# x2's token tiles 1 to 3 turned for the gate by VectorE and DMAs over DRAM instead of by TensorE

## The chip, the cores and the metric

One core of a Trainium2 chip runs the kernel. The metric is the device time of one execution in microseconds (us), as the median of several runs; lower is better.

## What is computed

One layer of a small transformer over 512 tokens (`SEQ`) of width 1024 (`D_MODEL`). Two attentions of 8 heads each are computed, normalised, gated and projected by `w_out`; the part that matters here comes after them:

```python
x = x + jnp.concatenate([y_sb, y_mb], axis=-1) @ w_out[i]
ple_gate = jax.nn.sigmoid(rmsnorm(x, g_ple[i]) @ w_ple_gate[i])
x = x + (p[i] @ w_ple[i]) * ple_gate
return rmsnorm(x, g_final)
```

The gate's matmul contracts over the 1024 features of x, so the features have to lie on partitions, while the sum in the line above it leaves the tokens on partitions. That turn of x is what the change is about.

## The kernel before

The 512 tokens are four tiles t = 0 to 3 of 128 tokens. `x2[0]` is one SBUF tensor `[128, 4, 1024]` (it prints as `x_2542`), tokens of a tile on partitions. Every matmul is made of three (`mul3`): both operands are split into a high and a low part in f32r, and high by high, high by low and low by high are accumulated in PSUM.

The kernel ends in this order:

- The output projection of the last heads. `out_step` fills a PSUM bank with half a tile (512 features), and `end_out` (line 422) adds it to `x2` on VectorE. The last three halves come from the generator `rest`: (tile 2, half 1) in a bank of the tag `tp`, (3, 0) and (3, 1) in the two banks that `bank()` gives out (`pj`, 2 buffers).
- Between them TensorE turns tile 0: `h2(0, 0)` and `h2(0, 1)`. `h2(t, c)` turns four blocks of 128 by 128 (`tr`, line 73: a TensorE transpose against the identity `idf`, into PSUM), and `split` makes the high part (`part_hi`, line 82, a cast on ScalarE) and the low part (`part_lo`, line 88, a subtraction on VectorE) of `H2[t]`, printed as `h`.
- The gate, tile by tile. `gate_steps` runs 24 matmuls of 128x512 for each half n of a tile (8 blocks k by 3) into a bank `pj`. After the first 12 of them `h2(t + 1, n)` turns half of the next tile. `end_gate` takes the sigmoid on ScalarE (line 890, out of PSUM, which frees the bank) and on VectorE multiplies by the loaded `pl` (line 891) and adds to `x2` (line 894). Then tile t is normalised and stored (lines 923 and 158).
- Tile 3 is cut into 512, 256 and 256 columns, and the kernel ends with its normalisation and its store.

TensorE runs in the order of the program text. ScalarE, VectorE, GpSimd and SP (SyncE, which issues all loads by `load`, line 158) are put in order by a scheduler when the kernel is built; on the chip each engine runs its own list in that order, and an instruction that waits holds all that stand behind it. `raw` is a pool of three buffers of `[128, 1024]` f32 through which all weights are loaded; the gate's weights are the last to use it. `pl_d` is a DRAM tensor to which the kernel stores a product early and from which it reads `pl` back here.

```python
        for n in range(2):
            ps = bank()
            gate_steps(t, ps, range(4), n * S, (n + 1) * S)
            h2(t + 1, n)
            gate_steps(t, ps, range(4, KT), n * S, (n + 1) * S)
            end_gate(t, n * S, (n + 1) * S, ps, r, pt[n])
```

Of the kernel before, what the change touches and what calls it, by code (L numbers as in the profile page):

```python
# [8 lines left out]
F32 = mybir.dt.float32  # L9
F32R = mybir.dt.float32r  # L10
# [5 lines left out]
P = 128  # L16
S = 512
DM = 1024
KT = DM // P
# [4 lines left out]
NT = S // P  # L24
# [10 lines left out]
def layer(ctx, tc, x, xT, pT, w_qkz, w_v, gcols, g_final, w_out, w_ple, w_gate, out):  # L35
# [12 lines left out]
    nc = tc.nc  # L48

    cst = ctx.enter_context(tc.tile_pool(name="cst", bufs=1))  # L50
    raw = ctx.enter_context(tc.tile_pool(name="raw", bufs=3))
# [4 lines left out]
    at = ctx.enter_context(tc.tile_pool(name="at", bufs=2))  # L56
    dram = ctx.enter_context(tc.tile_pool(name="dram", bufs=1, space=bass.MemoryType.DRAM))
# [8 lines left out]
    def bank():  # L66
        return pp.tile([P, S], F32, name="pj", bufs=2)
# [4 lines left out]
    def tr(ps, src):  # L72
        nc.tensor.transpose(ps, src, idf)  # L73

    def mul3(ps, ah, al, bh, bl, start, stop):
        mm(ps, ah, bh, start, False)
        mm(ps, ah, bl, False, False)
        mm(ps, al, bh, False, stop)

    def part_hi(hi, src, scale=None):  # L80
        if scale is None:
            nc.scalar.copy(hi, src)  # L82
        else:
            nc.scalar.activation(hi, src, AF.Copy, scale=scale)  # L84

    def part_lo(hi, lo, src, scale=None):
        if scale is None:
            nc.vector.tensor_sub(lo, src, hi.bitcast(F32))  # L88
        else:
            nc.vector.scalar_tensor_tensor(lo, src, scale, hi.bitcast(F32), op0=OP.mult, op1=OP.subtract)  # L90

    def split(hi, lo, src, scale=None):
        part_hi(hi, src, scale)
        part_lo(hi, lo, src, scale)
# [10 lines left out]
    def pop_w():  # L105
        if wq:
            hi, lo = wq.popleft()
            hi()
            if pend:
                pend.pop(0)()  # L110
            pend.append(lo)
        elif pend:
            pend.pop(0)()
# [8 lines left out]
    def tick(w=True):  # L122
        if w:
            pop_w()
        if fq:
            pop_f()
        for e in list(late):
            e[0] -= 1
            if e[0] <= 0:
                late.remove(e)  # L130
                e[1]()
# [25 lines left out]
    def load(tile_, src):  # L157
        nc.sync.dma_start(tile_, src)  # L158
# [259 lines left out]
    x2 = [None]  # L418
# [345 lines left out]
    for h in range(2 * NH):  # L764
        if h == 0:
            front(0)
        else:
            b = h - 1
# [47 lines left out]
    b = 2 * NH - 1  # L816
# [44 lines left out]
    def rms2(t):  # L861
        junk = at.tile([P, DM], BF16, name="junk", tag="o")
        ss = sm.tile([P, 1], F32, name="ss")
        nc.scalar.activation(junk, x2[0][:, t, :], AF.Square, accum_out=ss)  # L864
        r = sm.tile([P, 1], F32, name="r2")
        rstd(r, ss, DM, 1)
        return r

    H2 = {}

    def h2(t, c):
        if c == 0:
            H2[t] = [at.tile([P, KT, P], F32R, name=f"h2{i}", tag="AC"[i]) for i in range(2)]
        tp = pp.tile([P, 4, P], F32, name="tp2", tag="tp", bufs=2)
        for k in range(4):
            tr(tp[:, k, :], x2[0][:, t, (4 * c + k) * P:(4 * c + k + 1) * P])
        split(H2[t][0][:, 4 * c:4 * c + 4, :], H2[t][1][:, 4 * c:4 * c + 4, :], tp)

    def gate_steps(t, ps, ks, a, b):
        n, a, b = a // S, a % S, (b - 1) % S + 1  # L880
        for k in ks:
            while k not in wg or (t == 0 and n == 0 and (wq or pend) and k == KT - 1):
                pop_w()
            mul3(ps[:, :b - a], H2[t][0][:, k, :], H2[t][1][:, k, :], wg[k][n][0][:, a:b], wg[k][n][1][:, a:b],
                 k == 0, k == KT - 1)
            tick()

    def end_gate(t, a, b, ps, r, pt, between=None):
        gs = at.tile([P, S], F32, name="tmp")
        nc.scalar.activation(gs[:, :b - a], ps[:, :b - a], AF.Sigmoid, scale=r)  # L890
        nc.vector.tensor_mul(gs[:, :b - a], gs[:, :b - a], pt)
        if between:
            between()
        nc.vector.tensor_add(x2[0][:, t, a:b], x2[0][:, t, a:b], gs[:, :b - a])
# [10 lines left out]
    flush_late()  # L905
    while wq or pend:
        pop_w()
    for t in range(NT - 1):
        r = rms2(t)
        pt = [at.tile([P, S], F32, name="pl", tag="ph", bufs=2) for n in range(2)]  # L910
        for n in range(2):
            load(pt[n], pl_d[t, :, n * S:(n + 1) * S])
        for n in range(2):
            ps = bank()
            gate_steps(t, ps, range(4), n * S, (n + 1) * S)
            h2(t + 1, n)
            gate_steps(t, ps, range(4, KT), n * S, (n + 1) * S)
            end_gate(t, n * S, (n + 1) * S, ps, r, pt[n])
        r3 = rms2(t)
        for n in range(2):  # L920
            ns = slice(n * S, (n + 1) * S)
            ot = at.tile([P, S], F32, name="ot", tag="plo", bufs=2)
            nc.vector.scalar_tensor_tensor(ot, x2[0][:, t, ns], r3, gf[:, ns], op0=OP.mult, op1=OP.mult)
            load(out[t * P:(t + 1) * P, ns], ot)

    t = NT - 1
# [10 lines left out]
    def gate_cut(c, between=None):  # L937
        a, b = cuts[c]
        ps = bank()
        gate_steps(t, ps, range(KT), a, b)  # L940
        end_gate(t, a, b, ps, r, pt[a // S][:, a % S:a % S + b - a], between)
        return x2[0][:, t, a:b]
# [59 lines left out]
```

## Time and profile before

| | |
|---|---|
| time, median of 3 runs | 353.77 us (353.69 to 353.99) |
| time of the profiled execution | 353.86 us |
| its span, first to last instruction | 352.1 us |
| granted TensorE clock, mean | 0.993 |
| TensorE matmul (PE) busy | 343.4 us, 98% |
| TensorE weight load (PEld) busy | 287.4 us |
| VectorE (DVE) busy | 276.8 us, 79% |
| ScalarE (ACT) busy | 221.0 us, 63% |
| GpSimd (POOL) busy | 19.9 us, 6% |

The span is what the profile shows; the execution's own time is 1.76 us longer. Matmuls are pipelined: two that follow each other overlap in the records, so a stretch of them is read from start to start. PEld is the load of a matmul's weights, which runs beside the matmul ahead of it. SPq rows are DMA issues of SP.

### The profile page before, as it was taken

Reading aid. Unit: us, or ns where it says so; the run is one execution under the profiler, and the core shown is the slowest. Engines: PE = TensorE matmul, PEld = TensorE weight load, DVE = VectorE, ACT = ScalarE, POOL = GpSimd, SP = SyncE. Lnnn points to the kernel's source line nnn. Section 1 sums busy time; section 2 is a strip of 40 time slices with the busy share of each in tenths; the row PEclk is TensorE's granted clock in tenths of the full one; section 3 lists DMA queues with packets and bytes.
Section 4 is the critical chain, followed back from the end, with each engine's and each line's share of the span. In section 5 each row is a group of like instructions: output and inputs, shape, how many; then the busy total and the mean of one; then the engine's idle time right before and its main releaser. Section 6 shows DMA issues by size and latency. Waiting matters only on the chain.

```text
span 352.1 us, 4888 instructions
## 1 busy us (share of the span) xinstructions
PE 343.4 (98%) x1712; PEld 287.4 (82%) x1712; DVE 276.8 (79%) x564; ACT 221.0 (63%) x416; POOL 19.9 (6%) x43
## 2 busy tenths in 40 slices
PE   8999999999999999999999999999999999999991
PEld 7888888888888888888888888888888887888891
DVE  4887789788979797898489889989899877343554
ACT  4876857666766565685587499797776571343241
POOL 2023000000000000000000100000000010010011
PEclk9999999999999999999999999999999999999997
DMA  7997724303130313111005311122713750021221
GB/s 214 417 353 246 266 71 168 119 2 119 43 139 0 121 50 130 60 62 61 2 0 190 110 55 61 66 60 74 286 60 116 235 189 2 25 94 61 89 90 60
DMA packets 15464, 40.17 MB, mean 114 GB/s; under 512 B 1616, under 2 KB 1872, under 8 KB 15440
## 3 DMA queue, kind: packets, MB, share of 16 engines
q1 hardware_dynamic: 15296, 39.60, 32.1%
q8 instruction: 13, 0.21, 0.2%
q10 hardware_dynamic: 144, 0.26, 0.2%
q14 instruction: 11, 0.09, 0.1%
HBM read 35.66 MB, written 4.19 MB: 113 GB/s over the span
## 4 chain that ended last, share of the span: by engine, by line
PE 86%; DVE 4%; DMA 4%; issue 3%; ACT 1%; POOL 1%; SPq 0%; POOLq 0%; ACTq 0%; DVEq 0%
PE pj L70 64%; PE av L70 7%; PE sc L70 7%; PE tp L73 6%; DMA raw<-in_w_gate_dram 2%; PE tp L70 2%; DVE x L422 1%; DMA rawh<-in_pT_dram 1%; DVE wg L90 1%; POOL r L99 1%; SPq L158 0%; DVE wu L88 0%; ACT wg L84 0%; ACT junk L864 0%; POOLq L998 0%
## 5 line engine op out<-in xcount | busy, mean ns | idle before, releaser
L70 PE MATMUL pj<-hTh,wu 128*128 128x512 f32 x384 | 134.5, 401 | 0.0
L70 PEld LDWEIGHTS pj<-hTh,wu 128*128 128x128 f32 x384 | 72.2, 188 | 13.0
L70 PE MATMUL pj<-hTl,wu 128*128 128x512 f32 x192 | 75.1, 391 | 0.0
L82 ACT CAST wu<-raw 128x512 fp32r<-128x512 f32 x80 | 46.8, 619 | 24.7 <-PE pj L70 20.8
L88 DVE TENSOR_TENSOR wu<-raw,wu 128x512 fp32r<-128x512 f32 x80 | 53.3, 689 | 1.4 <-ACT wu L82 1.0
L70 PE MATMUL pj<-wg,h 128*128 128x512 f32 (+1 forms) x216 | 46.2, 371 | 0.0
L70 PEld LDWEIGHTS pj<-wg,h 128*128 128x128 f32 x216 | 37.0, 188 | 6.9
L70 PEld LDWEIGHTS pj<-hTl,wu 128*128 128x128 f32 x192 | 36.3, 189 | 5.1
L88 DVE TENSOR_TENSOR plo<-tp,ph 128x512 fp32r<-128x512 f32 (+1 forms) x48 | 28.5, 594 | 6.5 <-ACT ph L82 6.0
L82 ACT CAST ph<-tp 128x512 fp32r<-128x512 f32 (+1 forms) x48 | 24.5, 511 | 13.4 <-PE tp L73 13.3
L70 PE MATMUL pj<-wu,yh 128*128 128x512 f32 x96 | 30.9, 402 | 0.0
L70 PE MATMUL pj<-wu,hTh 128*128 128x512 f32 x96 | 30.1, 395 | 0.0
L621 DVE TENSOR_TENSOR_SCAN inc<-A,own 128x512 f32<-128x512 f32 (+3 forms) x32 | 24.7, 809 | 5.4 <-ACT A L616 5.4
L73 PEld LDWEIGHTS tp<-idf,C 128*128 128x128 f32 x160 | 20.4, 140 | 6.1
L73 PE MATMUL tp<-idf,C 128*128 128x128 f32 x160 | 25.2, 272 | 0.0
L70 PE MATMUL sc<-K,QH 128*128 128x512 f32 (+1 forms) x64 | 19.8, 323 | 0.0
L70 PEld LDWEIGHTS pj<-wu,hTh 128*128 128x128 f32 x96 | 17.3, 188 | 3.1
L70 PE MATMUL av<-ph,v 128*128 128x512 f32 (+1 forms) x64 | 19.7, 309 | 0.0
L658 ACT ACTIVATE C<-A,nm 128x512 f32<-128x512 f32 (+3 forms) x32 | 17.8, 558 | 3.1 <-DVE nm L654 3.0
L298 DVE TENSOR_TENSOR ev<-pj,rx 128x512 f32<-128x512 f32 x24 | 16.4, 684 | 3.9 <-PE pj L70 3.7
L70 PE MATMUL av<-plo,v 128*128 128x512 f32 (+1 forms) x64 | 19.1, 324 | 0.0
L70 PE MATMUL sc<-K,QL 128*128 128x512 f32 (+1 forms) x64 | 19.0, 323 | 0.0
(137 smaller groups left out, 557.2 us busy)
## 6 DMA issues: line engine op xcount, KB each, us to landing
raw<-in_w_qkz_dram SPq DMA_DIRECT2D x24, 512.0 KB, 3.4
raw<-in_w_v_dram SPq DMA_DIRECT2D x8, 512.0 KB, 3.3
raw<-in_w_out_dram SPq DMA_DIRECT2D x8, 512.0 KB, 3.7
raw<-in_w_gate_dram SPq DMA_DIRECT2D x8, 512.0 KB, 3.4
xt<-in_xT_dram SPq DMA_DIRECT2D x4, 512.0 KB, 7.5
xs<-in_x_dram SPq DMA_DIRECT2D x4, 512.0 KB, 10.6
pl_d<-pt SPq DMA_DIRECT2D x8, 256.0 KB, 5.7
x<-in_x_dram SPq DMA_DIRECT2D x4, 512.0 KB, 7.0
```

What stands on the lines that cost most here:

```text
L70: nc.tensor.matmul(ps, lhsT=lhsT, rhs=rhs, start=start, stop=stop)
L73: nc.tensor.transpose(ps, src, idf)
L82: nc.scalar.copy(hi, src)
L88: nc.vector.tensor_sub(lo, src, hi.bitcast(F32))
L90: nc.vector.scalar_tensor_tensor(lo, src, scale, hi.bitcast(F32), op0=OP.mult, op1=OP.subtract)
L99: nc.gpsimd.tensor_tensor(dst, t[:, :width], mhalf[:, :width], op=OP.pow)
L298: nc.vector.tensor_mul(t, ps, rx["all"])
L422: nc.vector.scalar_tensor_tensor(x2[0][:, t, ns], ps, r_o[half][:, t:t + 1], x2[0][:, t, ns], op0=OP.mult, op1=OP.add)
L621: nc.vector.tensor_tensor_scan(inc[:, c:c + b - a][:, ::-1], keep[:, a:b][:, ::-1], own[:, S - (b - a):][:, ::-1], 0.0, op0=OP.mult, op1=O ...
L658: nc.scalar.activation(w[:, a:b], s[:, a:b], AF.Exp, scale=QKS, bias=nm[:, i:i + 1], accum_out=l[:, i:i + 1])
```

## The change

Tile 0 is turned as before. Tiles 1 to 3 lose their TensorE transposes: `h2(t + 1, n)` gives way to `h2_turned(t + 1, n)`, which makes the high and low part from an SBUF tensor that already holds the turned tile. That tensor is made by `turn(t)`: two VectorE instructions turn each block of 32 by 32 in its place (every group of 32 partitions by itself) and sort the blocks by the group that they must go to; one DMA stores the result `yb` to a DRAM tensor `y_d`, and four DMAs read it back, each for 32 partitions, as `xb`. The runs in each are of 256 f32. `yb` and `xb` come from the pool `raw`. `turn(1)` stands ahead of the gate loop, `turn(t + 2)` behind the first half of tile t.

```diff
+    def turn(t):
+        y, tt = (raw.tile([P, DM], F32, name=n, tag="raw") for n in ("yb", "xb"))
+        yv = y.rearrange("p (b k j) -> p k b j", b=4, j=32)
+        for n in range(2):
+            nc.vector.transpose(yv[:, 4 * n:4 * n + 4], x2[0][:, t, n * S:(n + 1) * S].rearrange(
+                "p (k b j) -> p k b j", b=4, j=32))
+        y_d = dram.tile([P, DM], F32, name=f"y_d{t}")
+        load(y_d, y)
+        src = y_d.rearrange("(a i) (b c) -> b i a c", a=4, b=4)
+        for b_ in range(4):
+            load(tt[32 * b_:32 * b_ + 32, :].rearrange("i (a c) -> i a c", a=4), src[b_])
+        turned[t] = tt.rearrange("p (a k j) -> p k a j", a=4, j=32)
+
+    turned = {}
+
+    def h2_turned(t, c):
+        if c == 0:
+            H2[t] = [at.tile([P, KT, P], F32R, name=f"h2{i}", tag="AC"[i]) for i in range(2)]
+        ks = slice(4 * c, 4 * c + 4)
+        hi, lo = (H2[t][i][:, ks, :].rearrange("p k (a j) -> p k a j", a=4) for i in range(2))
+        split(hi, lo, turned[t][:, ks])
...
     while wq or pend:
         pop_w()
+    turn(1)
     for t in range(NT - 1):
...
             gate_steps(t, ps, range(4), n * S, (n + 1) * S)
-            h2(t + 1, n)
+            h2_turned(t + 1, n)
+            if n == 0 and t + 2 < NT:
+                turn(t + 2)
             gate_steps(t, ps, range(4, KT), n * S, (n + 1) * S)
```

The scheduler places the new instructions. On VectorE, around the end of the output projection, the list before reads (`x_2542<-tp` adds half (2, 1), `x_2542<-pj` halves (3, 0) and (3, 1) to `x2`; `h_3050` is tile 0's low part):

```order
L422 SCALAR_TENSOR_TENSOR x_2542<-tp,r_2967,x_2542 128x512 [waits PE_49]
L88 TENSOR_TENSOR h_3050<-tp_3051,h_3049 128x512 [waits Activation_49]
L98 TENSOR_SCALAR rs_t<-ss 128x1
L422 SCALAR_TENSOR_TENSOR x_2542<-pj,r_2967,x_2542 128x512 [waits PE_49]
L88 TENSOR_TENSOR h_3050<-tp_3072,h_3049 128x512 [waits Activation_49]
L422 SCALAR_TENSOR_TENSOR x_2542<-pj,r_2967,x_2542 128x512 [waits PE_49]
L88 TENSOR_TENSOR h_3117<-tp_3118,h_3116 128x512 [waits Activation_49]
L891 TENSOR_TENSOR tmp<-tmp,pl 128x512 [waits DMAHW3_49,Activation_49]
```

and with the change (lines 884, 914 and 917 are of the changed kernel; 914 and 917 were 891 and 894; `h_3127` is tile 1's low part):

```order
L422 SCALAR_TENSOR_TENSOR x_2542<-tp,r_2967,x_2542 128x512 [waits PE_49]
L88 TENSOR_TENSOR h_3050<-tp_3051,h_3049 128x512 [waits Activation_49]
L884 STREAM_TRANSPOSE yb<-x_2542 128x4x4x32 [waits DVE_49] x2
L98 TENSOR_SCALAR rs_t<-ss 128x1
L422 SCALAR_TENSOR_TENSOR x_2542<-pj,r_2967,x_2542 128x512 [waits PE_49]
L88 TENSOR_TENSOR h_3050<-tp_3072,h_3049 128x512 [waits Activation_49]
L422 SCALAR_TENSOR_TENSOR x_2542<-pj,r_2967,x_2542 128x512 [waits PE_49]
L884 STREAM_TRANSPOSE yb<-x_2542 128x4x4x32 [waits DVE_49] x2
L914 TENSOR_TENSOR tmp<-tmp,pl 128x512 [waits DMAHW3_49,Activation_49]
L917 TENSOR_TENSOR x_2542<-x_2542,tmp 128x512 [waits DVE_49]
L88 TENSOR_TENSOR h_3127<-xb,h_3126 128x512 [waits DMAHW2_49,DMAHW1_49,DMAHW3_49,DMAHW0_49,Activation_49]
L88 TENSOR_TENSOR h_3127<-xb,h_3126 128x512 [waits Activation_49]
```

Tile 1's two transposes stand ahead of the addition of half (3, 0), tile 2's behind that of half (3, 1), and both low parts of tile 1 come behind the end of tile 0's first half.

On SP the list before, from the second `pl` of tile 0 on, reads:

```order
L158 DMA pl<-pl_d 128x512 [waits PE_49]
L158 DMA pl<-pl_d 128x512 [waits DMAHW3_49,DVE_49]
L158 DMA pl<-pl_d 128x512 [waits DMAHW6_49,DMAHW0_49,DVE_49]
L158 DMA out_dram<-ot 128x512 [waits DVE_49]
L158 DMA out_dram<-ot 128x512 [waits DMAHW2_49,DVE_49]
```

and with the change (`y_d_3096` is tile 1's DRAM tensor, `y_d_3134` tile 2's):

```order
L158 DMA pl<-pl_d 128x512 [waits PE_49]
L158 DMA y_d_3096<-yb 128x1024 [waits DVE_49]
L158 DMA xb<-y_d_3096 32x4x256 [waits DMAHW4_49,DMAHW7_49,DMAHW0_49,Activation_49]
L158 DMA xb<-y_d_3096 32x4x256
L158 DMA xb<-y_d_3096 32x4x256 [waits DMAHW2_49]
L158 DMA xb<-y_d_3096 32x4x256 [waits DMAHW3_49]
L158 DMA y_d_3134<-yb 128x1024 [waits DVE_49]
L158 DMA pl<-pl_d 128x512 [waits DMAHW5_49,DVE_49]
L158 DMA xb<-y_d_3134 32x4x256 [waits DMAHW6_49,DMAHW4_49]
```

Tile 1's store and its four loads come at once behind the two `pl` of tile 0; the first load waits for the store. Tile 2's loads stand behind a `pl` of tile 1 that waits for line 914. Tile 3's store comes behind tile 0's two stores of the output, its loads behind that store and another `pl`, and the second `pl` of tiles 1 and 2 now stand behind the output stores of the tile ahead.

## Rows read from the trace of the kernel before

**Rows 1.** The page's first part: span, and busy time of each engine.

```profile
span 352.1 us, 4888 instructions
PE 343.4 (98%) x1712; PEld 287.4 (82%) x1712; DVE 276.8 (79%) x564; ACT 221.0 (63%) x416; POOL 19.9 (6%) x43
```

**Rows 2.** The page's fourth part: the chain that ended last, by engine.

```profile
PE 86%; DVE 4%; DMA 4%; issue 3%; ACT 1%; POOL 1%; SPq 0%; POOLq 0%; ACTq 0%; DVEq 0%
```

**Rows 3.** That chain in order of time, the gate: start us, us, what.

```profile
300.19 0.44 PE tp L73 x4
300.63 5.54 PE pj L70 x24
...
330.14 0.44 PE tp L73 x4
```

**Rows 4.** Timeline of TensorE in the gate: start us, us, instruction.

```profile
306.01 0.60 PE L73 MATMUL tp<-idf,x 128*128 128x128 f32 x4
...
312.00 0.60 PE L73 MATMUL tp<-idf,x 128*128 128x128 f32 x4
```

**Rows 5.** Windows: PE, PEld, DVE, ACT, POOL busy (instructions); clock, DMA share, GB/s.

```profile
306.00:312.00 6.00, 6.00 (x29) 4.90 (x28) 2.97 (x5) 1.55 (x3) 0.00 (x0) 1.00 0.13 45
312.00:318.00 6.00, 6.00 (x29) 4.90 (x28) 3.62 (x7) 3.07 (x6) 1.09 (x2) 1.00 0.35 130
```

**Rows 6.** Timeline from the output projection's end to the gate's start, VectorE and TensorE.

```profile
293.18 0.74 DVE L422 SCALAR_TENSOR_TENSOR x<-tp,r,x 128x512 f32<-128x512 f32 x1
...
293.84 0.68 DVE L88 TENSOR_TENSOR h<-tp,h 128x512 fp32r<-128x512 f32 x1
293.97 0.42 PEld L73 LDWEIGHTS tp<-idf,x 128*128 128x128 f32 x4 [0.55 <-DVE x L422]
...
294.43 0.14 DVE L98 TENSOR_SCALAR rs_t<-ss 128x1 f32<-128x1 f32 x1
294.49 0.74 DVE L422 SCALAR_TENSOR_TENSOR x<-pj,r,x 128x512 f32<-128x512 f32 x1
...
295.28 0.69 DVE L88 TENSOR_TENSOR h<-tp,h 128x512 fp32r<-128x512 f32 x1
...
297.02 2.74 PEld L70 LDWEIGHTS pj<-wg,h 128*128 128x128 f32 x12
```

**Rows 7.** Groups by line and form on VectorE: busy us, mean ns, idle before.

```profile
L88 DVE TENSOR_TENSOR h<-tp,h 128x512 fp32r<-128x512 f32 x8 | 5.5, 687 | 6.0 <-ACT h L82 5.9
...
L621 DVE TENSOR_TENSOR_SCAN inc<-A,own 128x512 f32<-128x512 f32 x4 | 4.9, 1222 | 2.5 <-ACT A L616 2.5
...
L666 DVE TENSOR_SCALAR C<-C,rl 128x512 f32<-128x512 f32 x8 | 3.9, 484 | 0.1
```

**Rows 8.** DMA issues of the whole run: count, KB each, median us to landing.

```profile
raw<-in_w_gate_dram SPq DMA_DIRECT2D x8, 512.0 KB, 3.4
...
xs<-in_x_dram SPq DMA_DIRECT2D x4, 512.0 KB, 10.6
pl_d<-pt SPq DMA_DIRECT2D x8, 256.0 KB, 5.7
...
pl<-pl_d SPq DMA_DIRECT2D x8, 256.0 KB, 2.6
out_dram<-ot SPq DMA_DIRECT2D x7, 256.0 KB, 2.0
```

**Rows 9.** Timeline at the end of tile 0: ScalarE, and issues of SP.

```profile
303.50 1.28 ACT L890 ACT_TABLE_LOAD   x1 [2.24 <-PE pj L70]
304.79 0.69 ACT L890 ACTIVATE tmp<-pj,r 128x512 f32<-128x512 f32 x1
...
306.23 5.01 SPq L158 DMA_DIRECT2D pl<-pl_d  x2
...
306.65 0.59 ACT L82 CAST h<-tp 128x512 fp32r<-128x512 f32 x1 [1.17 <-PE tp L73]
...
314.51 1.00 SPq L158 DMA_DIRECT2D out_dram<-ot  x2
```

## The prediction

> **What bounds the kernel.** I read the page's first part first: TensorE's matmuls are busy for 98% of the span, VectorE for 79%, ScalarE for 63% [rows 1]. The chain that ended last confirms it: 86% of it is TensorE's own work [rows 2]. What matters is the stage that is edited, so I read that chain in order of time through the gate. It never leaves TensorE there: 24 matmuls, 4 transposes, 24 matmuls, and so on, with no wait; the group of four transposes occurs six times, first at 300.19 and last at 330.14, each for 0.44 us [rows 3]. The windows of one tile say the same of the others: in 6.00 us TensorE is busy all the time, VectorE for 2.97 to 3.62, ScalarE for 1.55 to 3.07, the DMA engines for 13 to 35% [rows 5]. The granted clock there is 1.00, the upper level (2.4 GHz). So TensorE time that goes from this stage should shorten the kernel, as long as what replaces it stays in the other engines' gaps.
>
> **What is removed.** 24 transposes, six groups of four. From one group to the next is 312.00 - 306.01 = 5.99 us [rows 4]; the 24 matmuls of 128x512 between two groups take 5.54 of it [rows 3], 0.231 each. A group costs 0.44 us, six cost 6 x 0.44 = **2.64 us**, all on the path. They lie side by side with no other TensorE work to hide them, and the matmuls that stay don't change.
>
> **What is added on VectorE.** Two instructions of 128x512 f32 for each of three tiles. The trace has no 32 by 32 transpose. On operands of that size the quickest VectorE row is the scaling at 0.48 us, the slowest the scan at 1.22; the subtractions that move every element once take 0.69 [rows 7]. I take 0.69, since a transpose also reads and writes each element once and has one result per element; 0.48 and 1.22 are the bounds. Per tile that is 1.4 us against some 2.4 to 3.0 us in which VectorE idles in every 6 us [rows 5]; the sum is hidden, but the place of the first pair has to be checked.
>
> The first pair goes in behind tile 0's first low part and ahead of the addition of half (3, 0). That addition frees the PSUM bank into which the gate's first matmul writes. Before, it ran from 294.49 to 295.23, and TensorE came to the gate with its weight load at 297.02 [rows 6]. From a VectorE result to TensorE's start are about 0.05 us (293.18 + 0.74 = 293.92, start 293.97 [rows 6]). So the addition may be late by 297.02 - 0.05 - 295.23 = 1.74 us, that is 0.87 for each of the two transposes. At 0.69 it ends at 295.23 + 1.38 = 296.61, 0.36 us early: no stall. Tile 0's second low part follows it and ends about 295.97 + 1.38 = 297.35; TensorE wants it only after the 12 matmuls of the first four blocks, near 300. The second pair stands behind the addition of half (3, 1), where VectorE then waits for ScalarE anyway, the third behind tile 1's low parts. All of these are hidden.
>
> The Trainium skill, VectorE: DVE Perf Modes, section "The three transpose paths", has 311 ns for a VectorE transpose of 128x128 in bf16 and 390 ns for TensorE's; as an estimate, four such blocks would be 1.24 us where I take 0.69. The row on TensorE here is far below the page's (four in 0.44 us), and no run here yet shows the VectorE one. By the page's figure the second rival below would be the case, at about its upper price.
>
> **What is added on the DMA side.** For each tile one store of 512 KB and four loads of 128 KB. Tile 1 has the least time. Its transposes end at about 294.43 + 1.38 = 295.8, and SP issues the store. Rows near it: 256 KB to the output land in 2.0 us, 512 KB of weights in 3.4, and 256 KB to pl_d, eight in a row, in 5.7 [rows 8]. Nothing else is in flight, so I take 3.5: 299.3. SP then issues four loads; a pair of issues takes 1.00 us [rows 9], so four take at most 2, to 301.3. `pl` comes back from DRAM in 2.6 us [rows 8]: landed near 303.9. The nearest bounds are 2.0 + 2.0 + 2.0 (301.8) and 5.7 + 2.0 + 10.6 (314.1, with the slowest load of the trace, four of 512 KB queued).
>
> When is it wanted? Without the transposes tile 1's matmuls start 48 x 0.231 = 11.1 us behind 297.02, at 308.1. Ahead of them are one cast (0.59 [rows 9]) and one subtraction (0.69), and the low part is wanted only by the third matmul, 0.46 later; so the data must be there by 308.1 + 0.46 - 1.3 = about 307.3. **The slack is 3.4 us.** The casts also stand behind the table load and the sigmoid of tile 0's first half (1.28 + 0.69 [rows 9]), which now begin some 0.4 earlier, at about 303.1, and end near 305.1; VectorE then does its two steps of that half (to 306.5) and the low part (to 307.2), 1.4 us before the third matmul at 308.6. ScalarE's and VectorE's lists hold no work of TensorE's behind the new wait until tile 0's second half ends at 308.1, which is when its sigmoid is due.
>
> Tile 2's store is issued before a `pl` that waits for the multiplication behind the sigmoid (about 305.8), so its loads go out behind that, at 306 to 308, and land by 311; they are wanted near 318. Tile 3's store stands behind tile 0's output stores (314.51 before [rows 9]): landed by 318, loads out by 320, landed by 323; wanted near 329. The second `pl` of tile 1, now behind those output stores too, lands near 318 and is needed near 319; if it is late only VectorE waits, not the bank, which the sigmoid has freed. These moves cost nothing.
>
> **Sum.** -2.64 us and nothing against it. The profiled execution has 353.86 us, 0.09 over the median; its sum is 351.22, and from the median 353.77 - 2.64 = 351.13. I give **351.15 us**.
>
> **Rivals.**
> - VectorE is late with the bank. If a transpose takes more than 0.87 us, the gate's first matmul waits, once. At the slowest row, 1.22, the addition ends at 297.67 and TensorE starts 0.70 us late: 353.77 - 2.64 + 0.70 = 351.83. For it: the operation is not in the trace and margin is only 0.36 us. Against it: every row that passes 128x512 once is at or under 0.75, and the scan carries a value from element to element. By the skill's figure the wait would be 0.74, the time 351.87. Chance 11%.
> - The way over DRAM is late: slower. Tile 1's blocks arrive after 307.3 and TensorE stands. From 310 on the wait is longer than the 2.64 us gained. The bounds' far end, 314.1, gives a wait of 6.8 us and 353.77 - 2.64 + 6.8 = 357.9; 311 gives 354.8. For it: four loads for 32 partitions each in runs of 1 KB are a shape that the trace does not have, and one late transfer is enough. Against it: the DMA engines are idle around 300, and the read back of `pl` over DRAM takes 2.6. The Trainium skill's same section warns that a plain DMA whose access pattern does the transposing is many times slower than one through the transpose hardware when the innermost stride is large. By that warning this rival would be the likely one; but the blocks are turned ahead of the DMA and its runs of 256 f32 stay contiguous, and no run here shows either case yet. Chance 5%.
> - The gain is eaten, no change. The same wait of 2 to 3.3 us, or TensorE meeting a second wait in each tile (casts behind the sigmoid instead of in the middle of a tile). Time 353.1 to 354.4. Against it: 1.4 us of slack in the tightest list, more in tiles 2 and 3. Chance 4%.
>
> **Range and chances.** The forecast has 80%, within 350.9 to 351.4 (2.4 to 2.8 us of gain with the runs' spread). With the first rival added the range is **350.9 to 352.0**, and under 1 in 10 is left out. A difference under 0.2% (0.7 us) can't be told from no change here. Faster 0.91 (the forecast and the first rival), same 0.04, slower 0.05.
>
> **What would show it.** In the changed profile TensorE's gate should run as one row of matmuls from 297 to about 342 with no transposes after 294, the bank's addition ending before 297.0, VectorE transposes near 0.69, the four loads of tile 1 landed by about 304 and no TensorE wait on DVE, ACT or DMA at the start of a tile. A wait at 297 with longer transposes is the first rival; a wait at 308 on ACT's cast with a DMA behind it is the second. The forecast is wrong if TensorE stands anywhere in the gate for over 0.3 us, or if matmuls without transposes between them run slower than 0.231.

## The result, and the profile after

The changed kernel takes **351.85 us** (median of 4 runs, 351.3 to 352.3), the kernel before beside it on the same chip 353.88 us; the ratio is 0.9942, 95% interval 0.9925 to 0.9959. In two later series on other occasions it took 351.51 us against 354.42 (ratio 0.9912, 0.989 to 0.9934) and 351.54 against 354.54 (0.9912, 0.9894 to 0.993). So the change makes the kernel faster, by 2.0, 2.9 and 3.0 us of the medians where 2.64 were forecast. The profiled execution has 352.3 us, the longest of its four.

The first two lines of the page, beside [rows 1], and the chain by engine, beside [rows 2]:

```profile
span 350.5 us, 4873 instructions
...
PE 341.8 (98%) x1688; PEld 285.1 (81%) x1688; DVE 279.6 (80%) x570; ACT 220.6 (63%) x416; POOL 19.6 (6%) x43
...
PE 92%; issue 2%; DMA 2%; ACT 1%; DVE 1%; SPq 0%; POOL 0%; POOLq 0%; DVEq 0%; ACTq 0%
```

24 matmuls less (1712 to 1688), six VectorE instructions more (564 to 570, 2.8 us more of busy time), and TensorE still fills 98%. The chain in order of time, as in [rows 3]: start us, us, what.

```profile
292.56 2.75 PE pj L70 x12
295.31 0.44 PE tp L73 x4
295.75 36.13 PE pj L70 x156
331.88 0.02 issue
331.90 0.70 ACT tmp L913
```

From 295.75 to 331.88, where the chain leaves TensorE for tile 2's end, stand 156 matmuls (the last 12 of the output projection and 144 of the gate) with nothing between them. The six groups of four transposes are gone and no wait has come in their place: 36.13 / 156 is 0.2316 each (0.231 before). The view of waits has no row for TensorE there.

The groups of VectorE between 290 us and the end, by form (busy us, mean ns, idle before), beside [rows 7]:

```profile
L884 DVE STREAM_TRANSPOSE yb<-x 128x512 f32<-128x512 f32 x6 | 3.9, 684 | 0.0
L88 DVE TENSOR_TENSOR h<-xb,h 128x512 fp32r<-128x512 f32 x6 | 3.9, 683 | 0.0
```

The new transpose takes 684 ns, the same as the subtraction from which its price was taken (687 before). The timeline around the gate's start (start us, us, engine, instruction), beside [rows 6]:

```profile
295.21 1.29 DVE L884 STREAM_TRANSPOSE yb<-x 128x512 f32<-128x512 f32 x2
296.43 0.11 DVE L98 TENSOR_SCALAR rs_t<-ss 128x1 f32<-128x1 f32 x1
296.46 0.74 DVE L422 SCALAR_TENSOR_TENSOR x<-pj,r,x 128x512 f32<-128x512 f32 x1
...
298.13 2.05 PEld L70 LDWEIGHTS pj<-wg,h 128*128 128x128 f32 x9
```

The pair takes 1.29 us. The addition that frees the bank ends at 296.46 + 0.74 = 297.20, and TensorE comes for the bank at 298.13, without a wait: 0.93 early, 0.57 and 0.60 in the two other profiles of the same kernel.

Tile 1's way over DRAM in the same timeline, from the store's issue on SP to the low parts on VectorE:

```profile
296.53 0.33 SPq L158 DMA_DIRECT2D y_d<-yb  x1
...
299.37 2.02 SPq L158 DMA_DIRECT2D xb<-y_d  x4
...
304.19 1.28 ACT L913 ACT_TABLE_LOAD   x1 [7.82 <-PE pj L70]
305.49 0.69 ACT L913 ACTIVATE tmp<-pj,r 128x512 f32<-128x512 f32 x1
306.07 1.13 ACT L82 CAST h<-xb 128x512 fp32r<-128x512 f32 x2
...
307.55 1.29 DVE L88 TENSOR_TENSOR h<-xb,h 128x512 fp32r<-128x512 f32 x2
```

The issues from 290 us on (count, KB each, median us to landing), beside [rows 8]:

```profile
y_d<-yb SPq DMA_DIRECT2D x3, 512.0 KB, 3.6
xb<-y_d SPq DMA_DIRECT2D x12, 128.0 KB, 2.8
```

The first load of tile 1 goes out 2.84 us behind its store, the fourth ends its issue at 301.39, and all twelve loads of `xb` landed within 2.5 to 3.4 us of their issue. The casts stand right behind the sigmoid with no wait on a DMA, and the low part is ready at 308.2 for a matmul near 309.9. The windows of one tile, beside [rows 5]:

```profile
306.00:312.00 6.00, 6.00 (x27) 4.88 (x26) 5.19 (x8) 1.91 (x5) 0.00 (x0) 1.00 0.44 131
312.00:318.00 6.00, 6.00 (x27) 4.87 (x26) 2.76 (x6) 3.89 (x7) 1.09 (x2) 1.00 0.37 127
```

TensorE is full in both and its granted clock stays at 1.00, the upper level. VectorE rises from 2.97 to 5.19 us in the first window, where it makes tile 1's low parts and turns tile 2, and it is still no bound.

**Where the time went.** Four stages of the profiled executions, in us, by TensorE's rows: the start of the eighth of the twelve matmuls `pj<-wp,pu`, with which TensorE's work on the inputs begins (the first part of the product p·w_ple, in two groups of six); from there to the gate's first matmul; the gate up to its last matmul's end; from there to the end of the span. The experiments below are in the same table.

| kernel | start | to the gate | gate | rest | span |
|---|---|---|---|---|---|
| before | 8.02 | 289.22 | 47.36 | 7.46 | 352.1 |
| the change | 9.28 | 289.08 | 44.76 | 7.39 | 350.5 |
| e1_same (the change) | 8.10 | 288.99 | 44.76 | 7.39 | 349.2 |
| e11_same (the change) | 8.73 | 289.18 | 44.76 | 7.40 | 350.1 |
| e2_room | 7.90 | 288.94 | 47.36 | 7.47 | 351.7 |
| e3_reuse | 8.10 | 289.92 | 46.68 | 7.39 | 352.1 |
| e4_noturn | 8.01 | 288.85 | 44.76 | 7.47 | 349.1 |
| e5_added | 8.36 | 288.95 | 47.36 | 7.41 | 352.1 |
| e6_after_plus2 | 8.76 | 290.61 | 44.82 | 7.41 | 351.6 |
| e7_before_plus2 | 8.74 | 288.93 | 47.36 | 7.48 | 352.5 |
| e8_late | 8.12 | 289.09 | 46.76 | 7.37 | 351.3 |
| e9_half0 | 8.28 | 288.36 | 44.76 | 7.18 | 348.6 |
| e10_later | 8.69 | 288.73 | 44.83 | 7.40 | 349.7 |

The gate lost 47.36 - 44.76 = 2.60 us. The profiled execution of the change gives 1.26 us of that back before the edit: the eighth matmul starts at 9.28 instead of 8.02. The first one starts between 3.93 and 4.16 in all thirteen profiles; what differs is how soon the later ones have their data. (The first expectations below call the eighth the first product's matmuls.) The chain at the start of the run (start us, us, what) shows why, of the kernel before and then of the change:

```profile
2.57 4.03 DMA rawh<-in_pT_dram
...
8.02 1.43 PE pj L70 x5
```
```profile
2.57 5.29 DMA rawh<-in_pT_dram
...
9.28 1.43 PE pj L70 x5
```

The same load of an input was issued at 2.57 in both and took 5.29 us instead of 4.03. The first two experiments ask whether the change causes that.

### The profile page after: what moved, and what is told of

It is laid out like the page before. It is cut to its first block, busy times and chain, and to the rows that moved or that the text cites. A ratio compares the mean times of both kernels' runs of the same rounds, so it can differ in the third digit from the quotient of the medians.

```text
span 350.5 us, 4873 instructions
## 1 busy us (share of the span) xinstructions
PE 341.8 (98%) x1688; PEld 285.1 (81%) x1688; DVE 279.6 (80%) x570; ACT 220.6 (63%) x416; POOL 19.6 (6%) x43
## 4 chain that ended last, share of the span: by engine, by line
PE 92%; issue 2%; DMA 2%; ACT 1%; DVE 1%; SPq 0%; POOL 0%; POOLq 0%; DVEq 0%; ACTq 0%
PE pj L70 67%; PE sc L70 9%; PE av L70 8%; PE tp L73 6%; PE tp L70 3%; DMA rawh<-in_pT_dram 2%; SPq L158 0%; ACT junk L864 0%; POOL r L99 0%; POOLq L1024 0%; DVE ot L949 0%; ACT ot L991 0%; DVE tmp L914 0%; DVE x L917 0%; DVE pu L88 0%
## 5 line engine op out<-in xcount | busy, mean ns | idle before, releaser
L70 PE MATMUL pj<-wg,h 128*128 128x512 f32 (+1 forms) x216 | 44.8, 368 | 0.0
```

The source lines that it names most:

```text
L70: nc.tensor.matmul(ps, lhsT=lhsT, rhs=rhs, start=start, stop=stop)
```

## The experiments

Theory A: the edit acts in the gate alone (2.6 us), and the start differs by chance from execution to execution. Theory B: the three new DRAM tensors slow the first loads, so about 1 us of the gain is lost at the start of every execution.

**e1_same.** The changed kernel once more, unedited.

> The changed kernel once more, word for word. The profile of the change showed the gate's stage shorter by 2.6 us, from the first gate matmul to the last (47.36 before, 44.77 now), and the first product's matmuls starting 1.26 us later, at 9.28 us instead of 8.02, because the first load of pT landed 5.29 us behind its issue instead of 4.03. Theory A (chance): how long the first loads take varies from execution to execution, of either kernel; then several executions spread over about 1 us, from 351.1 up, and the start of this profile lies anywhere from 8.0 to 9.3. Theory B (the three new DRAM tensors shift or slow the first loads): all executions start late, median 351.9 or more, start near 9.3. Under both the gate's stage is 44.8 with no wait of TensorE in it.

Measured: 351.51 us, ratio 0.9912 (0.989 to 0.9934). The start is at 8.10, the gate 44.76. The changed kernel can start as early as the kernel before, so the late start doesn't come with every execution of it.

**e2_room.** The kernel before with a DRAM tensor as much larger as the three new ones need; nothing reads or writes the room.

```diff
-    pl_d = dram.tile([NT, P, DM], F32, name="pl_d")
+    pl_d = dram.tile([NT + 3, P, DM], F32, name="pl_d")
```

> The kernel before with pl_d larger by three tiles of 512 KB that nothing touches: as much DRAM as the change takes, and nothing else of it. Theory A: as the kernel before, 353.8 (353.6 to 354.9 by the start's chance). Theory B: 0.7 to 1.3 us slower than before, 354.5 to 355.1, with its first matmuls at 9.3 instead of 8.0.

Measured: 354.07 us, ratio 0.999 (0.9972 to 1.0008), start 7.90. The larger DRAM tensor alone costs nothing. B as stated, about 1 us at every start, falls by the two runs together. Over all profiles in the table the start lies between 7.90 and 9.28. The eight with three new DRAM tensors or more lie between 8.10 and 9.28 (mean 8.54), the five without between 7.90 and 8.74 (mean 8.15): they overlap, but thirteen single executions can't exclude a few tenths of B. The times don't show it: e5_added below, with the three tensors, has 354.03 us beside 354.12 of the kernel before.

**e3_reuse.** The change, with a tensor that is there already in place of the new ones. The product p·w_ple that is kept in that tensor is overwritten in part (tile 0's `pl` is read behind the store of turned blocks), so the result is not the layer's.

```diff
-        y_d = dram.tile([P, DM], F32, name=f"y_d{t}")
+        y_d = pl_d[0]
```

> The changed kernel with the turned blocks stored into the first tile of pl_d, which has been read by then, instead of into three new DRAM tensors; tile 2's store then waits for tile 1's loads. Theory A: as the changed kernel, spread over 351.1 to 352.3. Theory B: 351.15, the first matmuls at 8.0 as before. Under both no wait of TensorE in the gate (44.8), as tile 2 has 9 us of slack.

Measured: 353.79 us, ratio 0.9975 (0.9957 to 0.9992), start 8.10. Both theories missed, because the one shared tensor ties stores, loads and `pl` to one another, and the scheduler made other lists out of that. TensorE's waits from 285 us on (waiting, released by: us in total, times, longest):

```profile
PEld pj L70 <- ACT h L82: 1.7, 1, 1.7
PEld tp L73 <- DVE x L422: 1.3, 1, 1.3
PEld pj L70 <- DVE h L88: 0.5, 1, 0.5
```

One of tile 1's transposes now stands ahead of the addition of half (2, 1), on which tile 0's TensorE transposes wait: 1.3 us. The other two stand at the start of tile 3, at 332.8. Its four loads were issued by 324.1 and each of the run's twelve landed within 3.7 us, but ScalarE's list has tile 3's casts behind the sigmoid of tile 2's second half (331.56), so the high part came 1.7 and the low part another 0.5 late. The blocks weren't late; the casts were listed late, which is the third rival's mechanism. The run says nothing on A or B, but it shows two places at which the change loses its gain when the order is another.

**e4_noturn.** The kernel before without the turn of tiles 1 to 3: nothing takes its place, and the gate reads the unturned tile, so the result leaves the turn out.

```diff
-        tp = pp.tile([P, 4, P], F32, name="tp2", tag="tp", bufs=2)
-        for k in range(4):
-            tr(tp[:, k, :], x2[0][:, t, (4 * c + k) * P:(4 * c + k + 1) * P])
+        if t:
+            tp = x2[0][:, t, 4 * c * P:(4 * c + 4) * P].rearrange("p (k c) -> p k c", c=P)
+        else:
+            tp = pp.tile([P, 4, P], F32, name="tp2", tag="tp", bufs=2)
+            for k in range(4):
+                tr(tp[:, k, :], x2[0][:, t, (4 * c + k) * P:(4 * c + k + 1) * P])
```

> The kernel before without the turn of tiles 1 to 3: high and low part are made from the unturned tile, so the output leaves that turn out. This is the 24 transposes alone, with nothing put in their place. If the six groups of 0.44 us are the whole gain, 353.8 - 2.6 = 351.15 and the gate's stage 44.75, as with the change (44.77): the replacement is hidden entirely. If the replacement costs something (a rival), this one is quicker than the change by what it costs, 0.3 us or more. Theory A: its start varies too, 8.0 to 9.3; theory B: it starts at 8.0 in its profile and its median is 351.15, below the change's 351.85.

Measured: 352.06 us, ratio 0.992 (0.9895 to 0.9946), and the gate at 44.76 us, the same as with the change. Its chain has the same unbroken row:

```profile
294.25 36.13 PE pj L70 x156
```

The removal alone is worth what the change is worth; the VectorE and DRAM way costs nothing that the profile shows.

**e5_added.** The other half by itself: the change with TensorE's transposes kept. The turned tiles are made, stored and loaded, and not read.

```diff
-            h2_turned(t + 1, n)
+            h2(t + 1, n)
```

> The changed kernel with TensorE's 24 transposes kept: VectorE's transposes, the stores to DRAM and the loads back are all issued, but the turned tile is not used; high and low part come from TensorE's transposes as before. This is the added work alone. Theory A (all that is added is hidden): as the kernel before, within 0.3 us, and the gate's stage 47.3 from the first gate matmul to the last (47.36 before). A rival, that the added work costs something on VectorE's or SP's list which the removed transposes only pay for: slower than before by 0.4 to 1 us, with a wait of TensorE on DVE or ACT in the gate.

Measured: 354.03 us, ratio 0.9991 (0.9968 to 1.0014), the gate at 47.36 us, no wait of TensorE from 285 us on. A piece of its chain, of which there are six, and the group of the transposes:

```profile
300.26 0.44 PE tp L73 x4
300.69 5.54 PE pj L70 x24
```
```profile
L884 DVE STREAM_TRANSPOSE yb<-x 128x512 f32<-128x512 f32 x6 | 4.0, 689 | 0.0
```

The additions are free beside TensorE's transposes too. e4 and e5 together: all of the gain is the 24 transposes, none of the cost is on the path.

**e6_after_plus2 and e7_before_plus2.** The margin at the bank, measured: two more VectorE instructions of 128x512 that read the bank of half (3, 0) ahead of its addition, in the change (e6) and in the kernel before (e7).

```diff
+    def end_rest(ps, t, n):
+        if (t, n) == (3, 0):
+            for _ in range(2):
+                more = at.tile([P, S], F32, name="more", tag="tmp")
+                nc.vector.scalar_tensor_tensor(more, ps, r_o[1][:, t:t + 1], x2[0][:, t, :S],
+                                               op0=OP.mult, op1=OP.add)
+        end_out(ps, 1, t, n)
+
...
-            after(1, lambda ps=ps, t=t, n=n: end_out(ps, 1, t, n))
+            after(1, lambda ps=ps, t=t, n=n: end_rest(ps, t, n))
```

> The changed kernel with two more instructions of VectorE that read the bank of half (3, 0) ahead of its addition and write a scratch tile; the scheduler puts them and tile 0's second low part ahead of the addition, 2 x 0.66 + 0.66 = 1.97 us. In the profiles of the change the addition ends 0.5 to 0.9 us ahead of TensorE's first weight load of the gate. If the place of tile 1's transposes is the tight one, as the prediction has it, TensorE now waits there for VectorE by 1.97 - 0.9 to 1.97 - 0.5 = 1.1 to 1.5 us. If the bank is not what TensorE waits for, no wait there.

> The same two instructions in the kernel before, where the addition ended 1.74 us ahead of what TensorE needs and the list behind it is the same. TensorE waits 1.97 - 1.74 = 0.2 us (0 to 0.4), about 1.3 us less than in the changed kernel: the two transposes of 0.645 that the changed kernel has there. If the wait is as long as in the changed kernel, the transposes do not use up that slack.

Measured in e6: a wait of 1.50 us, at the place that the first rival names. The row of the weight load puts it down to "issue"; the matmul behind it names the addition, for 1.11 us. The timeline of VectorE and TensorE:

```profile
296.58 1.39 DVE L849 SCALAR_TENSOR_TENSOR more<-pj,r,x 128x512 f32<-128x512 f32 x2
297.90 0.67 DVE L88 TENSOR_TENSOR h<-tp,h 128x512 fp32r<-128x512 f32 x1
298.50 1.39 DVE L422 SCALAR_TENSOR_TENSOR x<-pj,r,x 128x512 f32<-128x512 f32 x2
299.34 0.76 PEld L70 LDWEIGHTS pj<-wg,h 128*128 128x128 f32 x4 [1.50 <-issue]
299.37 0.94 PE L70 MATMUL pj<-wg,h 128*128 128x512 f32 x3 [1.11 <-DVE x L422]
```

The additions of halves (3, 0) and (3, 1) are one row here; the first begins at 298.50 instead of 296.58. It is 1.92 us later, because the scheduler put tile 0's second low part (0.60 of it) ahead of it too. Of those 1.92 some 0.4 were margin and 1.5 became a wait. In e7 there is no wait, where 0.2 us (0 to 0.4) was expected:

```profile
296.58 0.74 DVE L422 SCALAR_TENSOR_TENSOR x<-pj,r,x 128x512 f32<-128x512 f32 x1
...
297.44 2.74 PEld L70 LDWEIGHTS pj<-wg,h 128*128 128x128 f32 x12
```

The same two and the low part stand in front, and the addition ends at 296.58 + 0.74 = 297.32 for a weight load at 297.44. So before the change the bank had room for these three instructions, with 0.1 us to spare; the change puts two there itself, and what is left is 0.4 us here, 0.6 to 0.9 in its own profiles. There is one execution of each (353.38 and 354.27 us); the waits, not the times, carry this.

**e8_late.** The way over DRAM made later: tile 1 is stored three times, and the loads read the last copy.

```diff
+        for i in range(2 if t == 1 else 0):
+            load(dram.tile([P, DM], F32, name=f"y_e{i}"), y)
```

> The changed kernel with tile 1's block tile stored to DRAM three times (two copies go to DRAM tensors that nobody reads) ahead of its loads: the blocks land about 2 x 1.4 = 2.8 us later, at some 307. The scheduler, which expects the delay too, now puts tile 1's casts behind the sigmoid of tile 0's second half. Theory (the way over DRAM is hidden by slack, and late data shows as TensorE waiting for ACT's cast at the start of tile 1): the cast runs at about 310.4 instead of 306.1, TensorE waits 1.8 to 2.3 us at the start of tile 1 and nowhere else in the gate; the gate's stage is 46.6 to 47.1 instead of 44.77. If the casts' place is not what decides, the stage stays 44.8.

Measured: the gate at 46.76 us, 2.00 more than the change, in one execution of 353.1 us. The timeline of SP, ScalarE and TensorE, then TensorE's waits:

```profile
302.87 1.75 SPq L158 DMA_DIRECT2D xb<-y_d  x4
...
308.60 0.69 ACT L915 ACTIVATE tmp<-pj,r 128x512 f32<-128x512 f32 x1 [3.58 <-PE pj L70]
309.18 1.13 ACT L82 CAST h<-xb 128x512 fp32r<-128x512 f32 x2
...
309.84 0.30 PEld L70 LDWEIGHTS pj<-wg,h 128*128 128x128 f32 x2 [1.78 <-ACT h L82]
```
```profile
PEld pj L70 <- ACT h L82: 1.8, 1, 1.8
PEld pj L70 <- DVE h L88: 0.5, 1, 0.5
```

Counted from the gate's first matmul (297.21 here, 298.36 in the change), the loads go out at 5.7 us instead of 1.0; 2.8 us of delay were expected. The scheduler now lists the casts behind the sigmoid of tile 0's second half, which itself waits for TensorE; tile 1's first weights come 1.78 us late, and the low part holds TensorE for another 0.5. That is the third rival's mechanism, at the place that it names; 4.7 us more of delay ate 2.0 of the 2.6 us gained. The second rival's, TensorE standing because the blocks themselves land late, isn't shown: the last load was issued by 304.6 and none of the run's twelve took over 3.7 us to land, so the blocks were there by 308.3, before the sigmoid at 308.60, and the casts show no wait on a DMA.

**e9_half0, e10_later and e11_same.** Two ways further, beside the changed kernel. e9 turns tile 0's second half by VectorE and DRAM too (one transpose, a store of 256 KB and four loads of 64 KB, as in `turn`):

```diff
+        with tc.high_priority():
+            nc.vector.transpose(y.rearrange("p (b k j) -> p k b j", b=4, j=32), x2[0][:, 0, S:].rearrange(
+                "p (k b j) -> p k b j", b=4, j=32))
...
-    h2(0, 1)
...
+    split(H2[0][0][:, 4:, :].rearrange("p k (a j) -> p k a j", a=4),
+          H2[0][1][:, 4:, :].rearrange("p k (a j) -> p k a j", a=4), turned[0])
```

e10 only moves `h2(0, 1)` behind the last 12 matmuls of the output projection, right ahead of the gate.

> The changed kernel, with the second half of tile 0 turned by VectorE and DRAM too: four TensorE transposes less, one VectorE transpose, one 256 KB store and four 64 KB loads more. Theory (the way over DRAM is hidden wherever its slack is over some 7 us): 0.44 us gone, and with it the wait of about 0.5 us that some executions show on those transposes, so 0.3 to 1.0 us under the changed kernel, near 350.9. The half is wanted by the 13th matmul of the gate, about 300; VectorE turns it near 291, store landed near 294, four loads out by 296 and landed near 298: about 2 us of slack. Rival (the blocks come late, or VectorE's list is behind with the bank): one TensorE wait on ACT L82 at about 299 to 302 of up to 2 us, time 352 to 353.5, no faster than the changed kernel.

> The changed kernel, with the transposes of tile 0's second half moved behind the last 12 matmuls of the output projection, right ahead of the gate. Theory: the wait of TensorE on DVE x L422 at about 294, 0.5 us in some executions, is gone, and the transposes cost the same 0.44; 0 to 0.5 us under the changed kernel. Rival: the wait only moves, since tile 0's second half is now cast later (the 13th matmul of the gate wants it 2.8 us after the transposes; cast 0.6 and subtraction 0.7 behind VectorE's list of transposes, 1.3): 0 to 0.5 us over the changed kernel, with a TensorE wait on DVE h L88 near 300.

> The changed kernel once more, beside the two on the same chip. If its start differs from execution to execution by chance, its profile shows the real product's first matmul anywhere from 8.0 to 9.3 us, the gate stage at 44.7 to 44.8 us all the same, and its time 2.0 to 2.9 us under the kernel before.

Measured on one chip: e9 351.22 us, ratio to the kernel before 0.9899 (0.9879 to 0.9918); e10 351.42, 0.9904 (0.9886 to 0.9923); e11 351.54, 0.9912 (0.9894 to 0.993). The intervals overlap, so the times don't separate the three; the stages do. e9's chain, and its one cast of the turned half:

```profile
290.89 0.44 PE tp L73 x4
291.33 38.83 PE pj L70 x168
```
```profile
295.62 0.62 ACT L82 CAST h<-xb 128x512 fp32r<-128x512 f32 x1 [3.67 <-DMA xb<-y_d]
```

168 matmuls without a break, and the stretch to the gate takes 288.36 us instead of 288.99 to 289.18: 0.6 to 0.8 us less, of which 0.44 are the transposes. Their wait on VectorE (0, 0.27 and 0.31 in the three profiles of the change) covers part of the rest; up to 0.3 is not accounted for. The half was turned at 289.31 and could be cast at 295.62, 6.3 us later; the gate wants it 12 matmuls (2.8 us) after 296.64, at 299.4. e9 beats both kernels by the one trace, and the kernel before by its time. In e10 the four transposes cost 0.44 as ever, the wait at 294 is gone (to the gate 288.73), and no new one has come:

```profile
297.23 0.44 PE tp L73 x4
297.67 33.34 PE pj L70 x144
```

e11 began at 8.73, in the middle of the spread.

## Why the prediction was right

**The sum.** 24 transposes at 0.44 us a group made 2.64; the gate lost 2.60 in all three profiles of the change and in e4. The view that gave it was the chain in order of time: the transposes stood bare on a path that never left TensorE, so their time came off in full. e4 and e5 show the two halves apart.

**VectorE's price.** 0.69 was taken from the subtraction of that size, between bounds of 0.48 and 1.22; measured 0.684. (The kernel before has a quicker row than 0.48, one cast at 0.43; nothing rests on it.) The argument (each element read and written once) held. The Trainium skill, VectorE: DVE Perf Modes, section "The three transpose paths", gives 311 ns for 128x128 in bf16, from which 1.24 us was estimated; this trace does not agree for 128x512 in f32, turned in blocks of 32 by 32, and the measurement decides. The first rival, which hung on this, did not come to pass. (It is the one that the prediction means where it says, by the page's figure, "the second rival below".) e6 shows that its mechanism is real.

**The bank.** 0.36 us of room was forecast; 0.93, 0.60 and 0.57 were measured. Of the profile with 0.57 (e1_same):

```profile
293.84 0.42 PEld L73 LDWEIGHTS tp<-idf,x 128*128 128x128 f32 x4 [0.27 <-DVE x L422]
...
295.55 0.73 DVE L422 SCALAR_TENSOR_TENSOR x<-pj,r,x 128x512 f32<-128x512 f32 x1
...
296.85 2.28 PEld L70 LDWEIGHTS pj<-wg,h 128*128 128x128 f32 x10
```

The forecast took 0.05 off for the way from VectorE to TensorE, the measured figures don't, and the pair cost 1.29 instead of 1.38; that is 0.14 of the 0.2 between them. The 0.93 goes with something else: the profile before has TensorE held for 0.55 us at 293.97 by VectorE [rows 6], as it is here for 0.27, so that both engines start level from that addition. In the change's first profile that wait is 0, and TensorE is further behind VectorE; so it is in e5_added, where the room is 0.93 too (296.15 to 297.08).

**The way over DRAM.** Store to first load: 3.5 forecast, 2.84 measured; four issues: 2, measured 2.02; landed near 303.9 in the clock of the kernel before, by 301.39 + 3.4 = 304.8 at the latest here, where all lies 1.1 us later. The casts came behind the sigmoid, as told, and the low part was ready 1.7 us before its matmul (1.4 forecast). e8 shows the other side: with the loads 4.7 us later the casts stand behind another sigmoid, and TensorE waits. The Trainium skill, VectorE: DVE Perf Modes, section "The three transpose paths", warns of plain DMAs that do the transposing by their access pattern. That price was not met, with blocks that VectorE had turned ahead; no run has a DMA do the turning itself, so the warning itself stays untested here.

**The time.** 351.15 was forecast, 351.85, 351.51 and 351.54 were measured: all inside 350.9 to 352.0, all above the forecast's own 350.9 to 351.4. So they lie in the part of the range that was added for the first rival, which did not happen: the mechanism was right, but that the upper end held them is luck. No term of the sum accounts for the difference; the stages say that the gate gave what it should. What was left out is a term ahead of the edit: the start, which lay anywhere from 7.90 to 9.28 us, while the sum was made from an execution that began early, at 8.02. The medians of the kernel before moved alike, from 353.77 to 354.54, and the ratios scatter on both sides of the forecast's 351.15 / 353.77 = 0.9926. How often an execution starts late was not measured, so this names the likely source and no size.

## What to carry to other kernels

Where the chain never leaves the bounding engine, count what stands bare on it and take it off in full, then give the replacement a place, a price from the nearest row and a slack on every list that it enters. Turning a 512 KB tile by VectorE and DRAM took about 9 us from the first transpose to data that can be cast (6.3 for half a tile), and cost TensorE nothing where its consumer lay further off than that. Two instructions more ahead of the bank's addition, with the low part that the scheduler put there too, cost 1.5 us (e6), and casts that the scheduler listed behind a later sigmoid cost 2 (e8, e3): look at the lists, not only at the sums. Before reading a difference of 1 us out of two profiled executions, compare them stage by stage: here 1.3 of 2.6 us seemed lost, and they were lost ahead of the edit.

## What was not expected of the hardware

One and the same load of an input, issued at 2.57 us in two executions, took 4.03 us in one and 5.29 in the other, and with it TensorE's eighth matmul moved by 1.26 us; over 13 profiles it lay between 7.90 and 9.28, with the change and without it. And VectorE's transposes of 128x512 f32 cost 684 ns, no more than a subtraction of that size (683).
